# A third matmul group on the first 128 tokens at each stage change, with a narrower small piece and another order of the first transfers

## The chip, the cores and the metric

One core of one Trainium2 chip runs the whole program. The metric is the device time of one execution in microseconds (us). Five engines work side by side, each on its own list of instructions, in order: TensorE (matmuls and transposes; its weight loads are listed as PEld), VectorE (DVE), ScalarE (ACT), GpSimd (POOL) and SyncE (SP, which here issues the transfers from HBM). A difference of about 0.3%, some 3.4 us, is what runs of this kernel can tell from no change.

## The reference

Two layers, each over 256 tokens of width 1024, all in fp32:

```
for l in range(2):
    h   = rms_norm(x, norm_mix_pre[l])
    mix = hybrid_mixer(h, w_in[l], ...)          # 4 branches, gates, w_branch, w_out
    x   = x + rms_norm(mix, norm_mix_post[l])
    h   = rms_norm(x, norm_ffn_pre[l])
    x   = x + rms_norm(swiglu(h, w_ffn_in[l], w_ffn_out[l]), norm_ffn_post[l])

def swiglu(h, w_in, w_out):
    g, up = split(h @ w_in, 2);  return (silu(g) * up) @ w_out
```

The mixer multiplies h by w_in once and cuts the product into the inputs of four branches: a state-space branch, a gated softmax attention (fox), a block attention (moba) and one with selected keys (dsa). Their outputs go through w_branch, are weighted by sigmoid(h @ w_gate + b_gate), summed, and multiplied by w_out.

## The kernel before

Nearly all of the time is matmuls against weights that come from HBM once. A *chunk* is 1 MB of raw fp32 weights in SBUF. Each half of a chunk is split in two: `split_hi` (L303) lets ACT write whi, the weights in TensorE's fp32r form, and `split_lo` (L123, `sub_lo`) lets DVE write wlo, the remainder. The activations are split likewise into hh and hl, and each product is three matmuls: hh by whi, hl by whi, hh by wlo.

The work is a list of *quanta* in an order written out by hand. There are two forms. In `add_b` the weights stand in the array and 256 token columns pass by: 24 matmuls of 128x256 a quantum. In `add_a` 128 tokens stand in the array (the halves t=0 and t=1 of the 256) and 512 weight columns pass by: two chunks (kh=0, kh=1), each for both halves, so four quanta (kh, t) of 12 matmuls. `add_rows` does w_out and w_ffn_out; its last rows run for t=0 first and then for t=1, so that t=0 is done early.

The loop at the end of the program (L1100 to L1121) goes through the list. For each quantum it issues the loads (`load_to`), then the whi of the quanta up to HA=3 places ahead (`split_ahead`), then the wlo up to LA=2 ahead, then the quantum's matmuls. A chunk's `early` adds to both look-aheads. A program's engines get their instructions in that order, so a split that is emitted before a norm stands before it on its engine.

A *stage change* (`boundary`) happens three times: mixer to FFN in layer 0 (about 357 to 380 us), FFN to mixer (549 to 570) and mixer to FFN in layer 1 (905 to 928). There the result of one stage passes a norm, is added to x, passes the next stage's norm and is transposed. This runs per half t. `head` squares on ACT (junk, poss, L219) and multiplies on DVE (ny<-a,gain, L222); `body` adds to x (L226), squares again on ACT (junk, pnss, L234), multiplies (L237), takes the reciprocal root on POOL (pnr, L204) and scales on DVE (ny<-ny,pnr, L240); `tail_half` transposes ny on TensorE (eight 128x128, L268), writes hh on ACT (L279) and hl on DVE (L123). The next stage's first quanta are (0,0), (1,0) on t=0, then t=1's transposes (`st["t1"]`, hung before the third quantum as its `pre`), then (0,1), (1,1) on t=1.

Other places: the small piece of w_in (ik, dt, ff, iw; 84 columns laid out over 128, so its whi and wlo tiles are zeroed on POOL, L301 and L311), the start of the program (L155, L156, L1081 to L1088: SP issues x, grows, cst, then the first half chunks), and the FFN's columns (`ga_post`, `g_post`, `u_post`), where the first 256 columns of g and of u are form a and the rest form b.

Of the kernel before, what the change touches and what calls it, by code (L numbers as in the profile page):

```python
# [9 lines left out]
F32 = mybir.dt.float32  # L10
# [49 lines left out]
    return c  # L60


NS4 = 26
TAIL = 6
MID = 1
STEP = 3
HA = 3
LA = 2


class Chunk:
    def __init__(self, loads, pieces, zero=False):
        self.loads = loads
        self.pieces = pieces
        self.zero = zero
        self.raw = None
        self.early = 0
        self.hi = [None] * len(pieces)
        self.lo = [None] * len(pieces)


class Quantum:
    def __init__(self, chunk, pieces, emit):
        self.chunk = chunk
        self.pieces = pieces
        self.emit = emit
        self.pre = None
        self.ends = False


@with_exitstack
def kernel(ctx: ExitStack, tc: tile.TileContext, a, out):
# [11 lines left out]
    def gps():  # L104
        return pg.tile([P, 512], F32, name="g")
# [190 lines left out]
    def split_hi(c, i):  # L296
        if c.hi[i] is not None:
            return
        c.hi[i] = s4.tile([P, 1024], F32R, name="whi", tag="s4", bufs=NS4)
        if c.zero:  # L300
            G.memset(c.hi[i].bitcast(F32), 0.0)  # L301
        for src, dst in c.pieces[i]:
            A.activation(dst(c.hi[i]), src(c.raw), AF.Copy)  # L303

    def split_lo(c, i):
        split_hi(c, i)
        if c.lo[i] is not None:
            return
        c.lo[i] = s4.tile([P, 1024], F32R, name="wlo", tag="s4", bufs=NS4)
        if c.zero:  # L310
            G.memset(c.lo[i].bitcast(F32), 0.0)  # L311
        for src, dst in c.pieces[i]:
            sub_lo(dst(c.lo[i]), src(c.raw), dst(c.hi[i]))

# [42 lines left out]
    def small_chunk(w):  # L357
        def blk(lo, hi):
            return lambda r: kcols(r[:, :KT * P], KT)[:, :, lo:hi]

        def wsrc(c0, n):
            return w[:, c0:c0 + n].rearrange("(k p) c -> p k c", p=P)
        loads = [(blk(0, 64), wsrc(COL["ik"], 64)), (blk(64, 72), wsrc(COL["dt"], 8)),
                 (blk(72, 80), wsrc(COL["ff"], 8)), (blk(96, 100), wsrc(COL["iw"], 4))]

        def src(r):
            return blk(0, 64)(r).rearrange("p k (two j) -> p k j two", two=2)

# [9 lines left out]
    def emit_b(hi, lo, kt, hh, hl):  # L378
        o = gps()[:, :S]
# [8 lines left out]
    def add_b(chunk, n, post):  # L388
        chunks.append(chunk)
        for j in range(n):  # L390
            def emit(j=j):
                return post(j, emit_b(kcols(chunk.hi[j], KT), kcols(chunk.lo[j], KT), KT, *h_act()))
            quanta.append(Quantum(chunk, [j], emit))

    def add_a(w, cols, post, by_token):
        cs = [a_chunk(w, kh, cols) for kh in range(2)]
        chunks.extend(cs)
        acc = {}
        qs = []
        for kh, t in [(0, 0), (1, 0), (0, 1), (1, 1)] if by_token else [(0, 0), (0, 1), (1, 0), (1, 1)]:  # L400
            def emit(kh=kh, t=t):
                hh, hl = st["h"][kh]
                if kh == 0:
                    acc[t] = gps()
                wh = [kcols(p, 2) for p in cs[kh].hi]
                wl = [kcols(p, 2) for p in cs[kh].lo]
                for pc in range(2):
                    for n, (h, w_) in enumerate(((hh, wh), (hh, wl), (hl, wh))):
                        for k in range(2):
                            mm(acc[t], h[:, 2 * pc + k, t * P:(t + 1) * P], w_[pc][:, k, :],  # L410
                               kh + pc + n + k == 0, kh + pc + n + k == 5)
                if kh:
                    return post(t, acc[t])
            qs.append(Quantum(cs[kh], [0, 1], emit))
        quanta.extend(qs)
# [92 lines left out]
    def mixer(l):  # L508
# [99 lines left out]
        def agemm(key, first=False):  # L608
            cs, qs = add_a(w, [COL[key]], v_post(key), first and l > 0)
            if first:  # L610
                cs[0].early = cs[1].early = 2
                if l:
                    qs[2].pre = st["t1"]
                else:
                    qs[1].pre, qs[2].pre = st["t1"]

        agemm("mv", True)
        agemm("fv")
        add_b(small_chunk(w), 1, small_post)
# [77 lines left out]
    def gates_gen(l, L, sraw):  # L697
        pt = aps()
        for t in range(2):
            T.transpose(pt[:, t * P:(t + 1) * P], sraw[:, t * P:(t + 1) * P], ident)  # L700
        yield
        pv = pt[:, 0:2 * P].rearrange("p (t c) -> p t c", t=2)

# [7 lines left out]
        V.tensor_scalar(L["w16"], pv[:, :, 96:100], 1.0 / 16, None, op0=ALU.mult)  # L711
# [251 lines left out]
    def ffn(l):  # L963
# [26 lines left out]
        def ga_post(t, o):  # L990
            yield
            g = tp.tile([P, S], F32, name="gt", bufs=5)
            A.activation(g, o[:, 0:S], AF.Silu)
            yield
            u = t1k("hu")
            V.tensor_tensor(u, g, o[:, S:2 * S], op=ALU.mult)
            yield
            pt = aps()
            for j in range(2):
                T.transpose(pt[:, j * P:(j + 1) * P], u[:, j * P:(j + 1) * P], ident)  # L1000
            yield
            qs = slice(t * P, (t + 1) * P)
            hid_of(0)
            hh, hl = H[0]
            pv = pt[:, :S].rearrange("p (k q) -> p k q", k=2)
            A.activation(hh[:, 0:2, qs], pv, AF.Copy)
            yield
            sub_lo(hl[:, 0:2, qs], pv, hh[:, 0:2, qs])
# [142 lines left out]
```

## Time and profile before

| | |
|---|---|
| three runs | 1118.28, 1115.13, 1118.37 us (median 1118.28) |
| the profiled execution | 1115.65 us, its span 1113.6 us |
| TensorE busy | 1094.3 us, 98% of the span |
| DVE, ACT, POOL busy | 712.2, 588.4, 239.0 us (64%, 53%, 21%) |
| the chain that ended last | 81% TensorE, 12% DVE, 2% ACT |
| HBM | 169 GB/s over the span |

TensorE is busy nearly all the time, so time can only be won where it waits or by giving it less to do. Matmuls overlap in TensorE and their ends are modelled, so a wait is best read at the weight load of the instruction that waited (engine PEld), where the row names in brackets how long the engine had nothing to do and which instruction released it. In a timeline the first number is the start, the second the busy time of the whole group of equal instructions.

### The profile page before, as it was taken

The numbers are of one execution on the slowest core, as the hardware profiler recorded it, in microseconds if no ns is written. First come the engines' busy times: TensorE is split into PE (matmuls) and PEld (weight loads), VectorE is DVE, ScalarE is ACT, GpSimd is POOL, SyncE is SP. The second block draws the span as 40 slices with busy tenths as digits, with TensorE's granted clock in tenths as the row PEclk, the third lists the DMA queues.
The fourth block names the chain that finished last, engine by engine and source line by source line (L and its number), as shares of the span: only waits on it lengthen the run. The fifth ranks groups of instructions, "written<-read, shape, count | busy, mean of one in ns | idle before, by whom it ended". The sixth has DMA issues, their size and how long they took to land.

```text
span 1113.6 us, 20105 instructions
## 1 busy us (share of the span) xinstructions
PE 1094.3 (98%) x8067; PEld 1013.4 (91%) x8067; DVE 712.2 (64%) x1324; ACT 588.4 (53%) x1084; POOL 239.0 (21%) x277
## 2 busy tenths in 40 slices
PE   7999999999999999999999999999999999999997
PEld 5998989999999899998879999899999988999986
DVE  6799857554556755456478996666555576555542
ACT  6546764665445554445355576655644455444541
POOL 1332347113232100000014333451223120000000
PEclk9999999999999999999999999999999999999999
DMA  7744543444548355646654445343455664555651
GB/s 229 230 152 140 164 152 119 149 149 152 190 156 291 121 190 162 199 170 227 227 146 132 152 152 190 114 152 120 147 160 181 214 202 153 194 184 185 217 185 38
DMA packets 153920, 188.94 MB, mean 170 GB/s; under 512 B 12740, under 2 KB 129764, under 8 KB 153828
## 3 DMA queue, kind: packets, MB, share of 16 engines
q1 hardware_dynamic: 153828, 187.67, 51.5%
q8 instruction: 63, 1.03, 0.4%
q14 instruction: 29, 0.24, 0.1%
HBM read 186.61 MB, written 1.05 MB: 169 GB/s over the span
## 4 chain that ended last, share of the span: by engine, by line
PE 81%; DVE 12%; ACT 2%; issue 2%; DMA 2%; POOL 1%; SPq 1%; DVEq 0%; POOLq 0%; ACTq 0%
PE g L120 61%; PE a L120 18%; DVE wlo L123 4%; DVE cacc L581 2%; DMA raw<-in_w_in_dram 2%; PE a L836 1%; ACT whi L303 1%; ACT junk L234 1%; DVE iacc L790 1%; DVE iacc L782 1%; DVE sm L814 1%; POOL pnr L204 1%; DVE rsh L499 1%; DVE m L789 1%; DVE ny L240 0%
## 5 line engine op out<-in xcount | busy, mean ns | idle before, releaser
L123 DVE TENSOR_TENSOR wlo<-raw,whi 128x1024 fp32r<-128x1024 f32 (+2 forms) x386 | 443.1, 1168 | 116.9 <-ACT whi L303 97.4
L303 ACT ACTIVATE whi<-raw 128x1024 fp32r<-128x1024 f32 (+2 forms) x386 | 367.5, 986 | 66.0 <-DMA raw<-in_w_ffn_out_dram 24.1
L120 PE MATMUL g<-hh,whi 128*128 128x256 f32 x1776 | 254.0, 286 | 0.0
L120 PE MATMUL g<-hl,whi 128*128 128x256 f32 x1776 | 249.3, 283 | 0.0
L120 PE MATMUL g<-hh,wlo 128*128 128x256 f32 x1776 | 249.2, 283 | 0.0
L120 PEld LDWEIGHTS g<-hh,whi 128*128 128x128 f32 x1776 | 227.9, 191 | 8.0 <-DVE rc L826 1.3
L120 PEld LDWEIGHTS g<-hh,wlo 128*128 128x128 f32 x1776 | 229.1, 192 | 0.0
L120 PEld LDWEIGHTS g<-hl,whi 128*128 128x128 f32 x1776 | 229.0, 192 | 0.0
L830 POOL TENSOR_SCALAR pr<-pr,rc 128x128 f32<-128x128 f32 x96 | 71.3, 754 | 153.8 <-DVE rc L826 131.8
L639 ACT ACTIVATE gt<-g,par 128x256 f32<-128x256 f32 x64 | 30.4, 475 | 118.4 <-PE g L120 118.4
L659 POOL TENSOR_TENSOR mg<-mg,gt 128x256 f32<-128x256 f32 x48 | 53.8, 1128 | 123.9 <-DVE gt L653 122.5
L150 POOL TENSOR_SCALAR gain<-gain 128x1024 f32<-128x1024 f32 x4 | 4.3, 1082 | 336.7 <-DMA gain<-in_norm_mix_pre_dram 157.7
L983 DVE TENSOR_TENSOR hu<-gt,g 128x256 f32<-128x256 f32 x40 | 16.8, 421 | 87.0 <-PE g L120 87.0
L120 PE MATMUL a<-whi,hidh 128*128 128x512 f32 x176 | 55.6, 390 | 0.0
L120 PE MATMUL a<-whi,hidl 128*128 128x512 f32 x176 | 55.5, 389 | 0.0
L120 PE MATMUL a<-wlo,hidh 128*128 128x512 f32 x176 | 55.5, 389 | 0.0
L975 ACT ACTIVATE gt<-g 128x256 f32<-128x256 f32 x40 | 15.4, 384 | 67.8 <-PE g L120 67.8
L502 POOL TENSOR_TENSOR rsh<-rsh,cst 128x256 f32<-128x256 f32 (+1 forms) x38 | 29.5, 775 | 93.6 <-DVE rsh L499 93.6
L653 DVE SCALAR_TENSOR_TENSOR gt<-gt,g 128x256 f32<-128x256 f32 x48 | 20.0, 419 | 44.5 <-PE g L120 38.5
L821 ACT ACTIVATE pr<-sm,mn 128x128 f32<-128x128 f32 x96 | 42.5, 447 | 7.5 <-DVE mn L814 7.5
L120 PE MATMUL g<-whi,hh 128*128 128x512 f32 x128 | 40.6, 399 | 2.4 <-ACT hh L274 1.7
L985 ACT ACTIVATE hidh<-hu 128x256 fp32r<-128x256 f32 x40 | 16.7, 418 | 45.3 <-DVE hu L983 45.3
(209 smaller groups left out, 1322.7 us busy)
## 6 DMA issues: line engine op xcount, KB each, us to landing
raw<-in_w_ffn_in_dram SPq DMA_DIRECT2D x40, 1024.0 KB, 5.2
raw<-in_w_in_dram SPq DMA_DIRECT2D x38, 1024.0 KB, 5.0
raw<-in_w_gate_dram SPq DMA_DIRECT2D x32, 1024.0 KB, 5.5
raw<-in_w_ffn_out_dram SPq DMA_DIRECT2D x22, 1024.0 KB, 4.9
raw<-in_w_branch_dram SPq DMA_DIRECT2D x16, 1024.0 KB, 5.1
raw<-in_w_in_dram SPq DMA_DIRECT2D x24, 512.0 KB, 6.2
raw<-in_w_out_dram SPq DMA_DIRECT2D x8, 1024.0 KB, 7.2
raw<-in_w_ffn_in_dram SPq DMA_DIRECT2D x8, 512.0 KB, 5.0
```

The lines of the kernel that those rows point to most:

```text
L120: T.matmul(o, l, r, start=start, stop=stop)
L123: V.tensor_tensor(lo, src, hi.bitcast(F32), op=ALU.subtract)
L303: A.activation(dst(c.hi[i]), src(c.raw), AF.Copy)
L502: G.tensor_tensor(sh[:n], sh[:n], sin[:n], op=ALU.mult)
L581: V.scalar_tensor_tensor(ac[:, sft:], u[:, :S - sft], wcol(3 - sft), ac[:, sft:], op0=ALU.mult, op1=ALU.add)
L639: A.activation(th, o, AF.Tanh, bias=par[:, l, 40 + br * 8 + d:41 + br * 8 + d], scale=0.5)
L653: V.scalar_tensor_tensor(L["gt", d], L["gt", d], 1.0, os[j], op0=ALU.add, op1=ALU.mult)
L659: G.tensor_tensor(md, md, L["gt", d], op=ALU.add)
L821: A.activation(pr[b][:, sl], sm[b][:, sl], AF.Exp, bias=mn[b][:, t:t + 1], scale=-1.0, accum_out=ls[b][:, t:t + 1])
L830: G.tensor_scalar(pr[b][:, sl], pr[b][:, sl], rc[b][:, t:t + 1], 1.0, op0=ALU.mult, op1=ALU.mult)
L983: V.tensor_tensor(u, H["s", j], o, op=ALU.mult)
L985: A.activation(hh, u, AF.Copy)
```

## The change

- At the three stage changes (not at the program's start) two groups of form a are emitted together by `begin`: (0,0) and (1,0) of the first group and (0,0) of the second on t=0, with t=1's transposes between the two halves of that third quantum (`mid`), then the five others. The second group's first chunk also has early=2, and the quanta of t=1 in `add_rows` load one chunk further (`after`).
- So the FFN's second 256 columns of g and u become form a instead of b. In mixer 1 the two groups are mv and fv, which were form a before.
- The small piece is 84 columns wide: its matmuls have 84 weight columns, its transposes 84 partitions; the zeroing is gone, and two of its three split pieces are one.
- At the start grows and the first part of cst are issued by ACT instead of SP, and the second half of x goes before the first chunk's second half.
- NS4, the number of 128x1024 tiles that whi, wlo, ny and others share, goes from 26 to 28.

```diff
-NS4 = 26
+NS4 = 28
+NSMALL = 84
-    nc.sync.dma_start(g_rows, a["norm_mix_pre"][0].rearrange("(k p) -> k p", p=P))
-    nc.sync.dma_start(cst[:, 0:P], a["cst"][:, 0:P])
+    nc.scalar.dma_start(g_rows, a["norm_mix_pre"][0].rearrange("(k p) -> k p", p=P))
+    nc.scalar.dma_start(cst[:, 0:P], a["cst"][:, 0:P])
...
-        if c.zero:
-            G.memset(c.hi[i].bitcast(F32), 0.0)
...
-                 (blk(72, 80), wsrc(COL["ff"], 8)), (blk(96, 100), wsrc(COL["iw"], 4))]
+                 (blk(72, 80), wsrc(COL["ff"], 8)), (blk(80, 84), wsrc(COL["iw"], 4))]
...
+    def group_a(w, cols, post):
...
+                    for pc in range(2):
+                        if pc and q.mid is not None:
+                            q.mid()
...
+    def begin(w, *groups):
+        (ca, qa), (cb, qb) = (group_a(w, *g) for g in groups)
+        chunks.extend(ca + cb)
+        quanta.extend([qa[0, 0], qa[1, 0], qb[0, 0], qa[0, 1], qa[1, 1], qb[0, 1], qb[1, 0], qb[1, 1]])
+        for c in (ca[0], ca[1], cb[0]):
+            c.early = 2
+        qb[0, 0].mid = st["t1"]
...
                 quanta[-1].ends = c == nch - 1
+                if t:
+                    quanta[-1].after = cs[-1]
...
+        if l:
+            begin(w, ([COL["mv"]], v_post("mv")), ([COL["fv"]], v_post("fv")))
...
-        cs, qs = add_a(w, [0, FFN], ga_post, True)
-        cs[0].early = cs[1].early = 2
-        qs[2].pre = st["t1"]
-        for c in range(1, FFN // S):
+        begin(w, ([0, FFN], ga_post(0)), ([S, FFN + S], ga_post(1)))
+        for c in range(2, FFN // S):
...
-    for step in "0 1 x 2 3".split():
+    for step in "0 x 1 2 3".split():
...
-        load_to(cidx[id(q.chunk)] + 3)
+        load_to(cidx[id(q.chunk)] + 3 if q.after is None else cidx[id(q.after)] + 4)
```

How this moves the instructions is seen at the first stage change. On ACT, from the squares of the old stage's t=0 to the first activation of the FFN (whi are the next chunks' splits, pnss the squares of the next norm, hh the activations after the transposes), before:

```order
L219 ACTIVATE junk,poss<-a 128x512 x2
L303 ACTIVATE whi<-raw 128x1024 x2
L234 ACTIVATE junk,pnss<-x 128x512 x2
L219 ACTIVATE junk,poss<-a 128x512
L279 ACTIVATE hh<-a 128x4x128 x2
L219 ACTIVATE junk,poss<-a 128x512
L234 ACTIVATE junk,pnss<-x 128x512 x2
L303 ACTIVATE whi<-raw 128x1024
L279 ACTIVATE hh<-a 128x4x128 x2
```

And after the change (line numbers are higher by two):

```order
L221 ACTIVATE junk,poss<-a 128x512 x2
L303 ACTIVATE whi<-raw 128x1024 x4
L236 ACTIVATE junk,pnss<-x 128x512 x2
L221 ACTIVATE junk,poss<-a 128x512
L281 ACTIVATE hh<-a 128x4x128 x2
L221 ACTIVATE junk,poss<-a 128x512
L236 ACTIVATE junk,pnss<-x 128x512 x2
L281 ACTIVATE hh<-a 128x4x128 x2
```

Two more whi stand ahead of t=0's squares, and the one ahead of t=1's hh is gone. On DVE, from t=0's addition to x to t=1's hl, before:

```order
L226 SCALAR_TENSOR_TENSOR x<-ny,por,x 128x512 x2
L237 TENSOR_TENSOR ny<-x,gain 128x512
L202 TENSOR_SCALAR pnm<-pnss 128x1
L237 TENSOR_TENSOR ny<-x,gain 128x512
L240 TENSOR_SCALAR ny<-ny,pnr 128x512 x2
L123 TENSOR_TENSOR wlo<-raw,whi 128x1024 x2
L222 TENSOR_TENSOR ny<-a,gain 128x512
L123 TENSOR_TENSOR hl<-a,hh 128x4x128 x2
L202 TENSOR_SCALAR pom<-poss 128x1
L222 TENSOR_TENSOR ny<-a,gain 128x512
```

After:

```order
L228 SCALAR_TENSOR_TENSOR x<-ny,por,x 128x512 x2
L239 TENSOR_TENSOR ny<-x,gain 128x512
L204 TENSOR_SCALAR pnm<-pnss 128x1
L239 TENSOR_TENSOR ny<-x,gain 128x512
L242 TENSOR_SCALAR ny<-ny,pnr 128x512 x2
L125 TENSOR_TENSOR wlo<-raw,whi 128x1024 x4
L224 TENSOR_TENSOR ny<-a,gain 128x512
L125 TENSOR_TENSOR hl<-a,hh 128x4x128 x2
L204 TENSOR_SCALAR pom<-poss 128x1
L224 TENSOR_TENSOR ny<-a,gain 128x512
```

Two more wlo stand between t=0's scaled ny and its hl. On TensorE, from the last matmuls of quantum (1,0) on, before:

```order
L120 MATMUL g<-wlo,hh 128x512 x2
L120 MATMUL g<-whi,hl 128x512 x2
L268 MATMUL a<-cst,ny 128x128 x8
L120 MATMUL g<-whi,hh 128x512 x2
L120 MATMUL g<-wlo,hh 128x512 x2
```

After, where a and cst are the transposes' output and identity:

```order
L122 MATMUL g<-wlo,hh 128x512 x2
L122 MATMUL g<-whi,hl 128x512 x2
L122 MATMUL g<-whi,hh 128x512 x2
L122 MATMUL g<-wlo,hh 128x512 x2
L122 MATMUL g<-whi,hl 128x512 x2
L270 MATMUL a<-cst,ny 128x128 x8
L122 MATMUL g<-whi,hh 128x512 x2
L122 MATMUL g<-wlo,hh 128x512 x2
```

Six more matmuls on t=0 stand ahead of t=1's transposes, and six more (the second half of the third quantum) between them and the first matmul that needs t=1's hh.

## Rows read from the trace of the kernel before

**Rows 1.** The chain that ended last: start us, us, what (x instructions)

```profile
275.55 72.18 PE g L120 x600
...
362.14 1.72 ACT whi L303 x2
...
367.58 2.27 DVE wlo L123 x2
...
895.98 13.64 PE a L120 x60
```

**Rows 2.** Busy time by windows: window, length, PE, PEld, DVE, ACT, POOL, clock, DMA, GB/s

```profile
100.00:120.00 20.00, 18.05 (x145) 16.56 (x145) 19.58 (x60) 15.47 (x40) 8.17 (x8) 1.00 0.49 158
357.00:380.00 23.00, 22.10 (x105) 17.87 (x104) 16.65 (x28) 12.07 (x25) 2.96 (x4) 1.00 0.40 129
560.00:575.00 15.00, 12.52 (x58) 9.80 (x57) 13.09 (x18) 7.50 (x14) 3.20 (x4) 1.00 0.27 42
905.00:930.00 25.00, 24.11 (x114) 19.48 (x113) 18.94 (x31) 13.80 (x27) 2.97 (x4) 1.00 0.39 126
```

**Rows 3.** Timeline of PEld, first stage change: start, busy, line, [wait, releaser]

```profile
367.77 1.02 PEld L268 LDWEIGHTS a<-cst,ny 128*128 128x128 f32 x8
...
371.10 0.30 PEld L120 LDWEIGHTS g<-whi,hl 128*128 128x128 f32 x2 [0.21 <-DVE hl L123]
...
376.58 0.86 PEld L268 LDWEIGHTS a<-cst,ny 128*128 128x128 f32 x8 [1.08 <-DVE ny L240]
377.93 0.30 PEld L120 LDWEIGHTS g<-whi,hh 128*128 128x128 f32 x2 [0.49 <-ACT hh L279]
```

**Rows 4.** Timeline of ACT, first stage change

```profile
362.04 2.00 ACT L303 ACTIVATE whi<-raw 128x1024 fp32r<-128x1024 f32 x2
363.94 0.62 ACT L234 ACTIVATE junk<-x 128x512 f32<-128x512 f32 x1
```

**Rows 5.** Timeline of DVE, first stage change

```profile
366.70 0.88 DVE L240 TENSOR_SCALAR ny<-ny,pnr 128x512 f32<-128x512 f32 x2 [0.45 <-POOL pnr L204]
...
370.37 1.28 DVE L123 TENSOR_TENSOR hl<-a,hh 128x512 fp32r<-128x512 f32 x2
...
376.04 0.88 DVE L240 TENSOR_SCALAR ny<-ny,pnr 128x512 f32<-128x512 f32 x2 [0.44 <-POOL pnr L204]
```

**Rows 6.** Timeline of PEld, second stage change

```profile
560.78 0.30 PEld L120 LDWEIGHTS g<-whi,hl 128*128 128x128 f32 x2 [0.25 <-DVE hl L123]
...
567.88 0.86 PEld L268 LDWEIGHTS a<-cst,ny 128*128 128x128 f32 x8 [2.65 <-DVE ny L240]
569.22 0.30 PEld L120 LDWEIGHTS g<-whi,hh 128*128 128x128 f32 x2 [0.49 <-ACT hh L279]
```

**Rows 7.** Timelines of DVE and POOL, second stage change

```profile
565.79 2.42 DVE L240 TENSOR_SCALAR ny<-ny,pnr 128x512 f32<-128x512 f32 x2 [0.44 <-POOL pnr L204]
...
565.70 0.95 POOL L301 MEMSET whi<- 128x1024 f32 x1
```

**Rows 8.** DMA issues of 352 to 356 us: count, KB each, us to landing

```profile
raw<-in_w_ffn_in_dram SPq DMA_DIRECT2D x1, 1024.0 KB, 7.2
```

**Rows 9.** Timeline of SP at the start: issue of transfers

```profile
1.63 0.37 SPq L155 DMA_DIRECT2D grows<-in_norm_mix_pre_dram  x1
...
2.43 0.94 SPq L294 DMA_DIRECT2D raw<-in_w_in_dram  x2
```

**Rows 10.** Timeline of ACT at the start

```profile
3.39 0.63 ACT L234 ACTIVATE junk<-x 128x512 f32<-128x512 f32 x1 [1.39 <-DMA x<-in_x_dram]
...
7.57 1.06 ACT L303 ACTIVATE whi<-raw 128x1024 fp32r<-128x1024 f32 x1 [2.68 <-DMA raw<-in_w_in_dram]
```

**Rows 11.** Timelines of DVE, POOL and PEld at the start, t=1's norm

```profile
12.88 1.78 DVE L257 TENSOR_SCALAR ny<-x,pnr 128x512 f32<-128x512 f32 x2 [0.67 <-POOL pnr L204]
...
13.04 0.95 POOL L301 MEMSET whi<- 128x1024 f32 x1
...
14.32 0.85 PEld L268 LDWEIGHTS a<-cst,ny 128*128 128x128 f32 x8 [1.46 <-DVE ny L257]
```

More of the change, by code (lines that the diff above doesn't have):

```diff
@@ L71, with __init__ @@
 class Chunk:
-    def __init__(self, loads, pieces, zero=False):
+    def __init__(self, loads, pieces):
         self.loads = loads
         self.pieces = pieces
-        self.zero = zero
         self.raw = None
@@ L87, in __init__ @@
         self.pre = None
+        self.mid = None
+        self.after = None
         self.ends = False
@@ L309, in split_lo @@
         c.lo[i] = s4.tile([P, 1024], F32R, name="wlo", tag="s4", bufs=NS4)
-        if c.zero:
-            G.memset(c.lo[i].bitcast(F32), 0.0)
         for src, dst in c.pieces[i]:
@@ L370, in dst @@
             return blk(0, 64)(r).rearrange("p k (j two) -> p k j two", two=2)
-        p1, p2 = blk(64, 80), blk(96, 100)
-        return Chunk(loads, [[(src, dst), (p1, p1), (p2, p2)]], zero=True)
+        p1 = blk(64, 84)
+        return Chunk(loads, [[(src, dst), (p1, p1)]])
     def h_act():
@@ L376, in h_act, with emit_b @@
         return (lambda k: hs[k // 4][0][:, k % 4, :]), (lambda k: hs[k // 4][1][:, k % 4, :])
-    def emit_b(hi, lo, kt, hh, hl):
-        o = gps()[:, :S]
+    def emit_b(hi, lo, kt, hh, hl, m=P):
+        o = gps()[:m, :S]
         for k in range(kt):
@@ L386, in emit_b, with add_b @@
         return o
-    def add_b(chunk, n, post):
+    def add_b(chunk, n, post, m=P):
         chunks.append(chunk)
@@ L391, in emit @@
             def emit(j=j):
-                return post(j, emit_b(kcols(chunk.hi[j], KT), kcols(chunk.lo[j], KT), KT, *h_act()))
+                return post(j, emit_b(kcols(chunk.hi[j], KT)[:, :, :m], kcols(chunk.lo[j], KT)[:, :, :m], KT,
+                                      *h_act(), m))
             quanta.append(Quantum(chunk, [j], emit))
-    def add_a(w, cols, post, by_token):
+    def group_a(w, cols, post):
         cs = [a_chunk(w, kh, cols) for kh in range(2)]
-        chunks.extend(cs)
[L398 to L415, printed above, removed]
-        return cs, qs
@@ new lines, in group_a, with emit, run @@
+        acc = {}
+        qs = {}
+        for kh in range(2):
+            for t in range(2):
+                def emit(q, kh=kh, t=t):
+                    hh, hl = st["h"][kh]
+                    if kh == 0:
+                        acc[t] = gps()
+                    wh = [kcols(p, 2) for p in cs[kh].hi]
+                    wl = [kcols(p, 2) for p in cs[kh].lo]
+                    for pc in range(2):
+                        if pc and q.mid is not None:
+                            q.mid()
+                        for n, (h, w_) in enumerate(((hh, wh), (hh, wl), (hl, wh))):
+                            for k in range(2):
+                                mm(acc[t], h[:, 2 * pc + k, t * P:(t + 1) * P], w_[pc][:, k, :],
+                                   kh + pc + n + k == 0, kh + pc + n + k == 5)
+                    if kh:
+                        return post(t, acc[t])
+                q = Quantum(cs[kh], [0, 1], None)
+                def run(emit=emit, q=q):
+                    return emit(q=q)
+                q.emit = run
+                qs[kh, t] = q
@@ new lines, in group_a, with add_a @@
+        return cs, qs
+    def add_a(w, cols, post):
+        cs, qs = group_a(w, cols, post)
+        chunks.extend(cs)
+        quanta.extend(qs[o] for o in ((0, 0), (0, 1), (1, 0), (1, 1)))
+        return cs, qs
+    def begin(w, *groups):
[5 more added lines that the diff above has]
+        qb[0, 0].mid = st["t1"]
@@ L514, in small_post @@
             sraw = t1k("sraw")
-            A.activation(sraw, o, AF.Copy)
+            A.activation(sraw[:NSMALL], o, AF.Copy)
             yield from rope(o[0:64], [(L["ik"][0:64], LOWER)], 64)
@@ L606, in bgemm, with agemm @@
                 add_b(cols_chunk(w, COL[key] + c * S, S, KT, perm), 2, post(2 * c))
-        def agemm(key, first=False):
-            cs, qs = add_a(w, [COL[key]], v_post(key), first and l > 0)
-            if first:
-                cs[0].early = cs[1].early = 2
-                if l:
-                    qs[2].pre = st["t1"]
[L614 to L619, printed above, removed]
+        def agemm(key):
+            return add_a(w, [COL[key]], v_post(key))
+        if l:
+            begin(w, ([COL["mv"]], v_post("mv")), ([COL["fv"]], v_post("fv")))
+        else:
+            cs, qs = agemm("mv")
+            cs[0].early = cs[1].early = 2
+            qs[0, 1].pre, qs[1, 0].pre = st["t1"]
+            agemm("fv")
+        add_b(small_chunk(w), 1, small_post, NSMALL)
         bgemm("iq", lambda b: rope_post("iq", b, lambda: start(index_gen(l, L)), 2), True, 2)
@@ L699, in gates_gen @@
         for t in range(2):
-            T.transpose(pt[:, t * P:(t + 1) * P], sraw[:, t * P:(t + 1) * P], ident)
+            T.transpose(pt[:, t * P:t * P + NSMALL], sraw[:NSMALL, t * P:(t + 1) * P], ident[:NSMALL, :NSMALL])
         yield
@@ L710, in gates_gen @@
         L["w16"] = tp.tile([P, 2, 4], F32, name="w16")
-        V.tensor_scalar(L["w16"], pv[:, :, 96:100], 1.0 / 16, None, op0=ALU.mult)
+        V.tensor_scalar(L["w16"], pv[:, :, 80:84], 1.0 / 16, None, op0=ALU.mult)
         flags.add(("w16", l))
@@ L988, in u_post, with ga_post, f @@
             return f
[L990 to L1008, printed above, removed]
-        cs, qs = add_a(w, [0, FFN], ga_post, True)
-        cs[0].early = cs[1].early = 2
-        qs[2].pre = st["t1"]
-        for c in range(1, FFN // S):
+        def ga_post(c):
+            def f(t, o):
+                yield
+                g = tp.tile([P, S], F32, name="gt", bufs=5)
+                A.activation(g, o[:, 0:S], AF.Silu)
+                yield
+                u = t1k("hu")
+                V.tensor_tensor(u, g, o[:, S:2 * S], op=ALU.mult)
+                yield
+                pt = aps()
+                for j in range(2):
+                    T.transpose(pt[:, j * P:(j + 1) * P], u[:, j * P:(j + 1) * P], ident)
+                yield
+                qs, ks = slice(t * P, (t + 1) * P), slice(2 * c, 2 * c + 2)
+                hid_of(0)
+                hh, hl = H[0]
+                pv = pt[:, :S].rearrange("p (k q) -> p k q", k=2)
+                A.activation(hh[:, ks, qs], pv, AF.Copy)
+                yield
+                sub_lo(hl[:, ks, qs], pv, hh[:, ks, qs])
+            return f
+        begin(w, ([0, FFN], ga_post(0)), ([S, FFN + S], ga_post(1)))
+        for c in range(2, FFN // S):
             add_b(cols_chunk(w, c * S, S, KT), 2, g_post)
```

## The prediction

> **What bounds the kernel now.** I read the chain of waits first. It is matmuls nearly throughout, back to back: 600 of 128x256 take 72.18 us, so 0.120 us each, and 60 of 128x512 take 13.64 us, so 0.227 us each [rows 1]. Where TensorE never waits, only less work helps; so I looked next, in the busy time by windows, for the places where it does wait [rows 2]. The three stage changes leave 23.00 - 22.10 = 0.90, 15.00 - 12.52 = 2.48 and 25.00 - 24.11 = 0.89 us idle. Mixer 0 has one more hole: 1.95 us in 100 to 120 us, where DVE is busy 19.58 of 20 us. The rest of the loss is at the two ends of the program.
>
> Then I read one stage change engine by engine. In the first, TensorE reaches t=0's transposes at 367.77 and does not wait. It waits 0.21 us for t=0's hl at 371.10, then 1.08 us for t=1's scaled ny and 0.49 us for t=1's hh [rows 3]. The reader is to see what the chain of waits goes through there: two whi on ACT at 362.14 (ahead of t=0's squares) and two wlo on DVE at 367.58 (ahead of t=0's hl) [rows 1]. So splits that stand ahead of the norm are on the path already; one more there is paid in full. That decides the forecast.
>
> **The change part by part.**
>
> *The splits of the third group, on t=0's chain.* The order lists show two more whi on ACT ahead of t=0's squares and two more wlo on DVE ahead of t=0's hl. A pair of whi takes 363.94 - 362.04 = 1.90 us [rows 4], a pair of wlo 2.27 us [rows 1]. ACT goes from the whi into the squares without a wait, so the squares come 1.90 us later, the scaled ny at 366.70 + 1.90 = 368.60 [rows 5]. t=1's rows say how soon transposes follow: 376.58 - 376.04 = 0.54 us [rows 3, 5]. So t=0's transposes can start at 369.14, where TensorE was ready at 367.77: a new wait of 1.37 us. DVE then runs four wlo instead of two, so t=0's hl starts 1.90 + 2.27 = 4.17 us later, at 374.54 instead of 370.37 [rows 5], and the matmul that waits for it moves from 371.10 to 375.27. This is 2.8 us more of waiting after the 1.37.
>
> *What the third group then covers.* t=1's chain stands behind these same instructions on DVE, so it is 4.17 us late too: its transposes can start at 376.58 + 4.17 = 380.75. From the hl matmul to the end of the two first quanta TensorE had 376.58 - 1.08 - 371.10 = 4.40 us of work [rows 3]; now it has six matmuls more, 6 x 0.227 = 1.36 us. It comes to the transposes at 375.27 + 4.40 + 1.36 = 381.03, and they are ready. The 1.08 us wait is gone. The transposes take 0.86 us; t=1's hh is ready 377.93 - 376.58 = 1.35 us after their start, and the 1.36 us of the second half cover it: the 0.49 us wait is gone too. t=1's first matmul starts at 381.03 + 0.86 + 1.36 = 383.25. By then 2.72 us of work is done that came later before. Against 377.93 the stage change costs 383.25 - 2.72 - 377.93 = +2.60 us.
>
> *The two other stage changes.* The third shows the same idle time as the first (0.89 against 0.90 us [rows 2]), so I put it at +2.60 as well. The second waits longer for t=1's ny, 2.65 us [rows 6], because DVE's scaling took 2.42 us instead of 0.88 while POOL zeroed the small piece's whi, from 565.70 on [rows 5, 7]; that zeroing goes. The hl matmul moves from 560.78 to 564.95; 567.88 - 2.65 - 560.78 = 4.45 us of work and 1.36 more end at 570.76; ny is ready at 565.79 + 0.54 + 4.17 = 570.50. So 570.76 + 0.86 + 1.36 - 2.72 - 569.22 = +1.04 us. Together +6.24 us. The bounds: if both pairs of splits fell into time in which nobody waits, the waits would go at no price, -1.57 - 3.14 - 1.57 = -6.3 us; if the next chunk came late as well, more than +6.24. I take the middle case as worked out, since the chain names both pairs' places.
>
> *The data for it.* The third transfer at 352 to 356 us, 1 MB of w_ffn_in, is issued at about 354.4 in the same place of SP's list and lands 7.2 us later [rows 8], near 361.6; ACT wants it at 363.94. Its cover is 2.3 us. If it is gone, each us late is a us of t=0's chain.
>
> *FFN columns.* 96 matmuls of 256 columns, 96 x 0.120 = 11.5 us, become 48 of 512, 48 x 0.227 = 10.9 us, with four transposes more (eight took 0.86 us [rows 3], so 0.43). Per FFN -0.2, together -0.4 us, between 0 and -1.2.
>
> *Start.* SP issued grows at 1.63 and the first half chunk at 2.43 [rows 9]; with grows and cst on ACT the half chunk goes 0.80 us sooner. ACT's first whi waited 2.68 us for it, to 7.57 [rows 10]. ACT's own two issues (as long as SP's, 0.37 us the one shown) fit before its first square at 3.39, which waited 1.39 us. I take -0.80 us, between 0 and -1.35. At t=1's norm the scaling took 1.78 us while POOL zeroed the same whi (13.04), and TensorE waited 1.46 us for it at 14.32 [rows 11]; without the zeroing 0.88, so -0.90, of which at least -0.3 should stay. Together -1.7, between -0.3 and -2.3. It reaches the end only through the stretch up to 120 us in which DVE is full; I take it that DVE's work starts sooner as well.
>
> The Trainium skill ("DMA: Bandwidth & Descriptors", section "Queues, rings and completion order") says that each DMA engine takes one ring's descriptors in ring order and goes round between the queues that have work. By that rule the first half chunk, behind x alone on SP's queue, would gain more than its 0.80, up to the 1.35 at which the hh before it decides, and the sum would be 0.55 us lower. Rows 10 do not tell: the wait for raw ends once only.
>
> *The rest.* 84 columns instead of 128: the same 24 matmuls of 256 moving columns, so nothing on TensorE; one split piece less per layer on ACT and DVE, and the smaller transposes, under 0.3 us. The 28 tiles cost nothing, and no row shows a wait for such a tile.
>
> The sum: +6.24 - 0.4 - 1.7 = +4.1 us, 1119.8 us against the profiled 1115.65. That execution lies below the median of the runs shown, 1118.28; from the median the sum gives 1122.4. I say 1122.
>
> **The rivals.**
>
> *A: the third group costs nothing and only fills.* Place: ACT at 362 and DVE at 367.5; the mechanism is that t=0's chain does not hang on its queue there (the additional splits run while ACT and DVE have nothing else, and DVE's hl is not needed in time). Then all waits of the three changes go: -6.3 - 0.4 - 1.7 = -8.4 us, 1110. It decides if TensorE came to t=0's transposes at least 1.4 us later than now, and to the first hl matmul 4 us later. For it speaks that TensorE's first chunk could wait for something else; against it, the chain of waits and the missing wait between whi and the square.
>
> *B: half of it.* Only ACT's pair delays, since the wlo turn out short or find a gap. Then the hl matmul comes at 373.00, the transposes at 378.76 against ready at 378.48, and the first and third change cost +0.33, the second -1.23: together -0.6, with the rest -2.7 us, 1115.6, within the bound. Against it: DVE runs its list in order, and hl stands behind the wlo in it.
>
> *C: the clock falls in the new waits.* The waits would be 1.4 and 2.8 us; the longest in these rows, 2.65 us, left the granted clock of its window at 1.00 [rows 2, 6], its upper level, 2.4 GHz. If it fell to 1.2 GHz for the 4.4 us that follow, each change would cost some 4.4 us more, +13 in all: 1135. The Trainium skill ("TensorE: Matmul & The Clock Gate", Part 1) has the slow clock as the default to which idleness leads back; the row at 2.65 us agrees with no fall there.
>
> *D: the start's gain is lost and the third chunk's data is late by 1 us.* +6.2 - 0.4 - 0.3 + 3 = +8.5: 1126.8. Slower as well.
>
> **How the numbers follow.** 0.3%, about 3.4 us, is what a measurement can tell from no change. The forecast has 0.55 with its own range 1119 to 1125, C 0.04, D 0.06, B 0.2, A 0.15. The forecast's +4.1 lies little above the bound: a fifth of its weight counts as the same. A and a fifth of B are faster: 0.19. The rest of B and that part of the forecast are within: 0.27. Slower: 0.54. The range leaves out C and the lower half of A and reaches from 1111 to 1126.
>
> **What would show it.** In the profile of the changed kernel, at each stage change: ACT runs four whi before t=0's squares; TensorE waits about 1.4 us at t=0's transposes for ny and about 3 us at the first hl matmul for hl; no wait at t=1's transposes nor at its first hh matmul; the granted clock stays at 1.00. At the second, DVE's scaling takes 0.88 us. At the start ACT's first whi is at about 6.8 us. If the new wait for hl is under 1 us, rival A or B is right and the forecast wrong; if ACT waits for raw before its third whi, D.

## The result, and the profile after

The changed kernel takes 1125.85 us (median of four runs, 1125.37 to 1127.39), the kernel before beside it 1118.13 us (1115.13 to 1118.37): a ratio of 1.0079, 95% interval 1.0063 to 1.0095. It is slower, and inside the range by 0.15 us, but by about twice what was forecast: +7.7 us between the medians, where the sum gave +4.1 and the 1122 that was stated is 3.7 above the median of before. On another chip (after_again below) it was 1.0076 (1.0061 to 1.0090).

The profiled execution took 1125.37 us with a span of 1123.6 us, 10.0 us longer than the one of before. Where it was lost can be read instruction by instruction, since both kernels load the same weights into TensorE in nearly the same order: the start of a load in the timeline of after, less the start of the same load in the timeline of before, is the delay gathered up to there. It is +0.54 us at 92 us, +2.04 from 140 us to the first stage change, +4.66 after it and the FFN's columns (at 407 us of before), +7.34 after the second stage change (at 596) and +9.93 after the third (at 980).

The first stage change on PEld, which answers to [rows 3]; ACT and DVE follow, which answer to [rows 4, 5]:

```profile
371.24 0.86 PEld L270 LDWEIGHTS a<-cst,ny 128*128 128x128 f32 x8 [1.46 <-issue]
...
377.31 0.30 PEld L122 LDWEIGHTS g<-whi,hl 128*128 128x128 f32 x2 [3.10 <-DVE hl L125]
...
383.13 1.02 PEld L270 LDWEIGHTS a<-cst,ny 128*128 128x128 f32 x8
...
385.38 0.41 PEld L122 LDWEIGHTS g<-whi,hh 128*128 128x128 f32 x2
```

```profile
364.08 3.89 ACT L303 ACTIVATE whi<-raw 128x1024 fp32r<-128x1024 f32 x4
367.87 0.62 ACT L236 ACTIVATE junk<-x 128x512 f32<-128x512 f32 x1
```

```profile
370.63 0.88 DVE L242 TENSOR_SCALAR ny<-ny,pnr 128x512 f32<-128x512 f32 x2 [0.45 <-POOL pnr L206]
371.43 4.62 DVE L125 TENSOR_TENSOR wlo<-raw,whi 128x1024 fp32r<-128x1024 f32 x4
375.97 0.68 DVE L224 TENSOR_TENSOR ny<-a,gain 128x512 f32<-128x512 f32 x1
```

The two waits that the kernel before had at t=1's transposes and at its first matmul (1.08 and 0.49 us) are gone: the rows at 383.13 and 385.38, the latter t=1's first matmul, have no bracket. In their place stand 1.46 us at t=0's transposes and 3.10 us at t=0's hl, because ACT spends 3.89 us on four whi and DVE 4.62 us on four wlo, where each had two. (The row with 1.46 us names no instruction that ended the wait; DVE's scaling of t=0's ny, at 370.63, stands 0.61 us ahead of it, and the wait is gone in a_noearly, whose splits stand elsewhere.)

The second stage change shows the same two waits, and DVE's scaling at 0.88 instead of 2.42 us [rows 6, 7]. But behind the wait the weight loads take 0.76 us a pair instead of 0.41, and the window's granted clock is 0.90, where the window of before had 1.00 [rows 2]. Weight loads on PEld, then the window (length, PE, PEld, DVE, ACT, POOL, clock, DMA share, GB/s):

```profile
563.49 0.86 PEld L270 LDWEIGHTS a<-cst,ny 128*128 128x128 f32 x8 [1.46 <-issue]
...
569.56 0.30 PEld L122 LDWEIGHTS g<-whi,hl 128*128 128x128 f32 x2 [3.10 <-DVE hl L125]
569.90 0.41 PEld L122 LDWEIGHTS g<-whi,hh 128*128 128x128 f32 x2
...
571.50 0.76 PEld L122 LDWEIGHTS g<-whi,hh 128*128 128x128 f32 x2
```

```profile
8.00:20.00 12.00, 10.37 (x33) 7.46 (x34) 9.03 (x19) 10.21 (x22) 0.81 (x2) 0.72 0.93 347
100.00:120.00 20.00, 18.03 (x133) 16.80 (x132) 19.58 (x58) 15.09 (x41) 8.17 (x8) 0.91 0.49 158
359.00:388.00 29.00, 25.27 (x119) 20.51 (x118) 20.08 (x31) 14.39 (x27) 2.97 (x4) 1.00 0.43 140
563.00:580.00 17.00, 13.82 (x61) 11.17 (x62) 12.82 (x20) 5.61 (x14) 1.41 (x2) 0.90 0.38 83
914.00:942.00 28.00, 24.27 (x115) 19.67 (x114) 19.62 (x30) 14.84 (x28) 2.96 (x4) 1.00 0.40 131
```

At the stage changes TensorE is idle 3.73, 3.18 and 3.73 us in these windows (0.90, 2.48 and 0.89 before). The granted clock was at its lower level, 1.2 GHz, for part of three windows: at the start (0.72), behind the hole at 111 us (0.91), and behind the second stage change (0.90). At the start ACT's first whi came no sooner (7.57 before [rows 10]) and its second one waits, though the first half chunk was issued at 1.63 instead of 2.43 us. DVE's scaling at t=1's norm takes 0.89 us instead of 1.78 [rows 11]. Issue on SP, ACT, DVE:

```profile
1.63 0.43 SPq L296 DMA_DIRECT2D raw<-in_w_in_dram  x1
...
7.77 1.06 ACT L303 ACTIVATE whi<-raw 128x1024 fp32r<-128x1024 f32 x1 [2.54 <-DMA raw<-in_w_in_dram]
...
10.43 1.06 ACT L303 ACTIVATE whi<-raw 128x1024 fp32r<-128x1024 f32 x1 [0.57 <-DMA raw<-in_w_in_dram]
...
13.77 0.89 DVE L259 TENSOR_SCALAR ny<-x,pnr 128x512 f32<-128x512 f32 x2 [0.67 <-POOL pnr L206]
```

### The profile page after: what moved, and what is told of

It reads as the page before. It is cut to its first block, busy times and chain, and to the rows that moved or that the text cites. A ratio compares the mean times of both kernels' runs of the same rounds, so it can differ in the third digit from the quotient of the medians.

```text
span 1123.6 us, 19946 instructions
## 1 busy us (share of the span) xinstructions
PE 1099.0 (98%) x7979; PEld 1013.6 (90%) x7979; DVE 709.1 (63%) x1322; ACT 587.6 (52%) x1082; POOL 233.1 (21%) x273
## 3 DMA queue, kind: packets, MB, share of 16 engines
HBM read 186.61 MB, written 1.05 MB: 167 GB/s over the span
## 4 chain that ended last, share of the span: by engine, by line
PE 88%; DVE 8%; ACT 2%; issue 1%; DMA 1%; POOL 0%; SPq 0%; DVEq 0%; POOLq 0%; ACTq 0%
PE g L122 67%; PE a L122 18%; DVE wlo L125 3%; DVE cacc L602 2%; PE a L856 1%; ACT whi L303 1%; DMA raw<-in_w_in_dram 1%; DVE iacc L810 1%; DVE sm L834 1%; DVE m L809 0%; PE a L270 0%; ACT junk L236 0%; DVE iacc L802 0%; DVE xsc L588 0%; POOL pnr L206 0%
## 5 line engine op out<-in xcount | busy, mean ns | idle before, releaser
L125 DVE TENSOR_TENSOR wlo<-raw,whi 128x1024 fp32r<-128x1024 f32 (+1 forms) x384 | 441.7, 1171 | 108.7 <-ACT whi L303 92.7
L303 ACT ACTIVATE whi<-raw 128x1024 fp32r<-128x1024 f32 (+1 forms) x384 | 366.5, 990 | 56.6 <-DMA raw<-in_w_ffn_out_dram 31.3
L122 PE MATMUL g<-hh,whi 128*128 128x256 f32 (+1 forms) x1712 | 245.3, 286 | 0.0
L122 PE MATMUL g<-hl,whi 128*128 128x256 f32 (+1 forms) x1712 | 241.0, 284 | 0.0
L122 PE MATMUL g<-hh,wlo 128*128 128x256 f32 (+1 forms) x1712 | 240.7, 283 | 0.0
L122 PEld LDWEIGHTS g<-hh,whi 128*128 128x128 f32 (+1 forms) x1712 | 219.6, 191 | 8.0 <-DVE rc L846 1.3
L122 PEld LDWEIGHTS g<-hl,whi 128*128 128x128 f32 (+1 forms) x1712 | 221.4, 192 | 0.0
L122 PEld LDWEIGHTS g<-hh,wlo 128*128 128x128 f32 (+1 forms) x1712 | 221.3, 192 | 0.0
L122 PE MATMUL g<-whi,hl 128*128 128x512 f32 x160 | 51.0, 401 | 8.0 <-DVE hl L125 8.0
L122 PE MATMUL g<-wlo,hh 128*128 128x512 f32 x160 | 51.2, 402 | 0.3 <-DVE wlo L125 0.2
```

What stands on the lines that cost most here:

```text
L122: T.matmul(o, l, r, start=start, stop=stop)
L125: V.tensor_tensor(lo, src, hi.bitcast(F32), op=ALU.subtract)
```

## The experiments

The theory after this result: the splits on t=0's chain cost what was forecast; each fall of the granted clock adds some 1.6 us; and the gain at the start does not exist or does not reach the end. The rivals stand in each expectation. The delays that the runs gathered against the profile of before, in us, by the method above (the columns are the stretches between 0, 92, 140, 407, 596 and 980 us of before; each row of a kernel is one profiled execution):

| kernel | start | 111 us | 1st change | 2nd | 3rd | end |
|---|---|---|---|---|---|---|
| forecast | -1.7 | 0 | +2.4 | +1.0 | +2.4 | +4.1 |
| changed | +0.54 | +1.50 | +2.62 | +2.68 | +2.59 | +9.93 |
| changed, again | +0.18 | 0.0 | +4.24 | +1.04 | +4.20 | +9.64 |
| a_fill | -0.19 | 0.0 | +2.60 | +1.04 | +2.56 | +6.01 |
| a_noearly | -0.45 | +1.69 | +0.48 | -0.97 | +0.44 | +1.20 |
| b_start | +0.87 | +1.46 | 0.0 | -0.64 | 0.0 | +1.69 |
| b_narrow | -0.44 | +0.19 | 0.0 | -1.29 | 0.0 | -1.51 |
| g1 | -0.74 | +1.69 | -1.56 | -3.09 | -1.61 | -5.31 |
| b_early | +0.22 | +1.66 | -0.14 | -1.31 | -0.17 | +0.26 |
| g2 | -0.12 | +0.19 | -1.58 | -3.07 | -1.59 | -6.16 |
| b_fill | +0.20 | +0.19 | 0.0 | +0.87 | 0.0 | +1.29 |

**The third group without its early splits (a_noearly).** Changed kernel, one line:

```diff
-        for c in (ca[0], ca[1], cb[0]):
+        for c in ca:
```

> The changed kernel, but the third group's first chunk has no additional look-ahead: its two whi come behind t=0's squares on ACT and its two wlo behind t=1's scaling on DVE. Theory (the splits on t=0's chain are the cost): TensorE waits neither for t=0's scaled ny nor over 0.3 us for t=0's hl; it waits some 2.1 us for wlo in the third quantum instead. First and third stage change +0.55 us each against the kernel before (the changed kernel has +2.6), the second -1.1 (it has +2.7, part of that the clock), no half clock at the second: 7.9 us less than the changed kernel, about 1118. Rival (the third group itself costs, by its order on TensorE or its PSUM): the stage changes keep their +2.6 and the time stays at 1125 to 1126.

Measured: 1117.23 us, ratio to before 1.0006 (0.9995 to 1.0017). TensorE's waits at the first stage change:

```profile
369.01 1.02 PEld L270 LDWEIGHTS a<-cst,ny 128*128 128x128 f32 x8
...
372.34 0.30 PEld L122 LDWEIGHTS g<-whi,hl 128*128 128x128 f32 x2 [0.21 <-DVE hl L125]
...
379.35 0.30 PEld L122 LDWEIGHTS g<-wlo,hh 128*128 128x128 f32 x2 [2.15 <-DVE wlo L125]
380.16 1.03 PEld L270 LDWEIGHTS a<-cst,ny 128*128 128x128 f32 x8
```

Both new waits are gone, and the wait for wlo that was expected at about 2.1 us is 2.15. The three stage changes gave +0.48, -0.97 and +0.44 us (expected +0.55, -1.1, +0.55). So the third group costs little by itself (the half microsecond left at the first and third is that wait for wlo); what the changed kernel lost there it lost by the place of two whi and two wlo.

**Matmuls that keep the clock up in the waits (a_fill).**

```diff
+                warm_up(5)
                 B[0].tail(st["h"])
...
+                            if q.fill and pc + (2 - n) == 0:
+                                warm_up(q.fill)
...
+        qa[0, 0].fill = 12
```

> The changed kernel with 5 idle-running bf16 matmuls ahead of t=0's transposes and 12 ahead of the first matmul with hl at each stage change: they fill about 1.1 of the 1.46 us and 2.6 of the 3.10 us in which TensorE waits, and nothing waits for them. Theory (the half clock after the second stage change comes from these waits): the granted clock stays at 1.00 there and the second stage change falls from +2.7 to about +1.0, the others stay at +2.6; 1124.2, 1.6 less than the changed kernel. Rival (the clock falls for another reason, or the fall costs nothing): clock and time as in the changed kernel, 1125.9.

Measured: 1122.35 us, ratio 1.0046 (1.0031 to 1.0061); the four mean granted clocks 0.997 to 0.999, where the changed kernel's first four were 0.993 to 0.995. The windows at the three stage changes (PE counts the idle matmuls as busy):

```profile
369.00:385.00 16.00, 15.93 (x79) 12.03 (x79) 13.53 (x21) 6.46 (x13) 1.48 (x2) 1.00 0.42 133
561.00:577.00 16.00, 15.93 (x79) 11.84 (x78) 13.04 (x21) 6.25 (x13) 1.41 (x2) 1.00 0.41 89
921.00:937.00 16.00, 15.94 (x78) 12.06 (x79) 13.54 (x21) 6.58 (x13) 1.48 (x2) 1.00 0.41 133
```

The clock is whole (1.00, never at its lower level) in this profile, and the second change costs +1.04 us, the forecast's number to the hundredth. The idle matmuls do nothing but run; t=0's hl is as late as in the changed kernel. So the falls at the stage changes come from the waits. By the ratios the filling is worth 0.3%, some 3.3 to 3.7 us, twice the 1.6 expected: an execution has one or two such falls, as the next run shows.

**The changed kernel again (after_again).** No edit.

> The changed kernel once more, unaltered, beside the others, for its own scatter. Theory (the waits at the stage changes cost the same each time, and the clock falls in some places only by the moment of the execution): the three stage changes again at +2.6, +1.0 (or +2.7 with a half clock behind it) and +2.6 against the kernel before; ratio about 1.007; mean granted clocks of 0.993 to 0.997. Rival (its first profile was a special one): stage changes that differ by more than 0.3 us where the clock is whole.

Measured: 1125.37 us, ratio 1.0076 (1.0061 to 1.0090). The stage changes did not cost the same again, for this time the second change had a whole clock and cost +1.04, and the first and third had a low one and cost 4.24 and 4.20 us:

```profile
370.00:385.00 15.00, 12.34 (x54) 9.84 (x52) 11.05 (x18) 4.49 (x11) 1.48 (x2) 0.89 0.45 141
569.00:584.00 15.00, 14.72 (x69) 12.27 (x70) 9.76 (x17) 6.56 (x13) 1.41 (x2) 1.00 0.41 110
922.00:940.00 18.00, 14.43 (x64) 11.64 (x64) 13.62 (x21) 6.59 (x14) 1.71 (x3) 0.91 0.36 117
```

Equal waits (1.46, then 3.10 us at all three places in both profiles) lower the clock in one place and not in another, from execution to execution; a fall costs 4.24 - 2.60 = 1.6 us. The hole at 111 us behaves alike: TensorE waits 2.08 to 2.34 us there in nine profiles, five of them have the low clock behind it and lose 1.46 to 1.69 us, and before has not, with 2.15 us. What decides it was not tested.

**The start alone (b_start).** The kernel before, with

```diff
-    nc.sync.dma_start(g_rows, ...    # and cst[:, 0:P]
+    nc.scalar.dma_start(g_rows, ...
-    for step in "0 1 x 2 3".split():
+    for step in "0 x 1 2 3".split():
```

> The kernel before with the start of the changed one alone: grows and cst issued by ACT, the second half of x ahead of the first chunk's second half. Theory (the transfers share one bandwidth, so the half chunk that is issued 0.8 us sooner lands no sooner, and its second half later): ACT's first whi at 7.6 to 7.8 us, the second about 1 us later than before, TensorE's unbroken stretch begins 0.5 to 1 us later, and the half clock appears in the first 20 us: the end is +0.6 to +2.5 us later than before by the span. Rival (a queue's transfers land in their order of issue): first whi at 6.8, the end 0.8 us sooner.

Measured: 1117.20 us, ratio 1.0004 (0.9993 to 1.0016): no difference that can be told. The profiles tell a little more. The first whi began at 7.77, 8.00, 7.67, 6.83 and 7.75 us in the five profiles with the new order, and at 7.57, 6.83, 6.37, 7.23, 6.59 and 6.52 in the six with the old: on the mean 7.60 against 6.85, with a scatter of 1.2 us within either set. So the half chunk that is issued 0.80 us sooner lands no sooner, and on the mean 0.75 us later. Its second half is late too, since x goes ahead of it:

```profile
7.75 1.06 ACT L303 ACTIVATE whi<-raw 128x1024 fp32r<-128x1024 f32 x1 [2.28 <-DMA raw<-in_w_in_dram]
...
10.43 1.06 ACT L303 ACTIVATE whi<-raw 128x1024 fp32r<-128x1024 f32 x1 [0.58 <-DMA raw<-in_w_in_dram]
```

The rival (landing in the order of issue, so the first whi at 6.8) has the order right and the time wrong. The loads of SP's queue do land as they were issued: in the changed kernel the first half chunk at 7.7 us, x at 9.1 and the second half chunk at 10.4 (1.63 + 6.1, 2.10 + 7.0 and 2.61 + 7.8, issue and time to landing), in the kernel before the two half chunks at 7.5 and 8.9 (2.43 + 5.1, 2.90 + 6.0). From 3 to 6 us the transfers moved 224 to 279 GB/s in the new order and 269 to 292 in the old; the one profile of the new order with 279 is the one whose first whi began at 6.83. Why the new order mostly moves less there was not tested. The half clock stood at 111 us in this profile, not at the start as expected.

**The narrow piece alone (b_narrow).** The kernel before, with NSMALL's edits and without the zeroing.

> The kernel before with the narrow small piece alone (84 columns, no zeroing on POOL, two split pieces instead of three). Theory (the zeroing on POOL slowed DVE's scaling): the scaling of t=1 at the start takes 0.88 instead of 1.78 us, at the second stage change 0.88 instead of 2.42, and TensorE's wait there falls from 2.65 to about 1.1 us: -1.5 us there, -0.9 us at the start if nothing else is late, together -2.4. Rival (something else is late behind it): less than 0.5 us gained in all.

Measured: 1115.80 us, ratio 0.9983 (0.9973 to 0.9993), a small gain. At the second stage change it is as expected: DVE's scaling takes 0.88 us, TensorE's wait is 1.14 instead of 2.65 us, and the change gives -1.29 us:

```profile
565.86 0.88 DVE L240 TENSOR_SCALAR ny<-ny,pnr 128x512 f32<-128x512 f32 x2 [0.44 <-POOL pnr L204]
...
566.40 0.86 PEld L268 LDWEIGHTS a<-cst,ny 128*128 128x128 f32 x8 [1.14 <-DVE ny L240]
```

Near 43 us TensorE ran 1.49 us ahead of before (0.74 of it because the first half chunk happened to land sooner, first whi at 6.83 instead of 7.57), and lost 1.05 of it in one new wait at 57 us, for the results that DVE makes there (sg), and more later:

```profile
57.32 0.55 PEld L120 LDWEIGHTS a<-cst,sg 128*16 128x16 f32 x6 [1.22 <-DVE sg L727]
...
111.18 0.52 PEld L120 LDWEIGHTS a<-mk,mq 64*128 64x128 f32 x6 [2.33 <-DVE mn L810]
```

This is the stretch in which DVE is full. A start that is sooner by 1.5 us is worth 0.25 behind it, so of the 2.4 us expected 1.5 are left at the end.

**The splits taken off the norm's chain (g1).** Changed kernel with the old start, and

```diff
-        for c in (ca[0], ca[1], cb[0]):
-            c.early = 2
+        ca[0].early, ca[1].early, cb[0].early = 2, 3, 1
...
-        for d, q in enumerate(quanta[i:i + ahead + 3]):
+        for d, q in enumerate(quanta[i:i + ahead + 4]):
```

The first group's second chunk is now split while ACT and DVE wait for t=0's last matmuls, and the third group's first chunk in the places that became free.

> The changed kernel with the start of the kernel before, and with the splits taken off the norm's chain: the first group's second chunk is split one quantum sooner (in time in which ACT and DVE wait for t=0's last matmuls), and the third group's first chunk has its whi behind t=0's squares and its wlo behind t=0's scaling. Theory (only the place of the splits made the change slow): TensorE waits at no transposes of the stage changes; -1.6, -3.1 and -1.6 us there against the kernel before, -0.2 per FFN, -0.2 of the start's -1.5 left: about -6.9 us, ratio 0.994. Rival 1 (the first group's second chunk lands too late for the sooner place: ACT waits for raw ahead of t=0's squares): 0 to +3 us a stage change. Rival 2 (the third group costs by itself): 0 or slower at each.

Measured: 1110.51 us (1109.43 to 1111.12), ratio 0.9941 (0.9928 to 0.9954): faster than the kernel before and than the changed one. The three changes gave -1.56, -3.09 and -1.61 us (expected -1.8, -3.1 and -1.8 with the columns), and TensorE is busy throughout:

```profile
357.00:380.00 23.00, 23.00 (x111) 19.08 (x110) 18.51 (x30) 11.80 (x25) 2.97 (x4) 1.00 0.59 194
559.00:575.00 16.00, 16.00 (x75) 13.16 (x75) 10.63 (x18) 7.39 (x15) 1.41 (x2) 1.00 0.34 103
901.00:926.00 25.00, 25.00 (x120) 20.75 (x119) 20.50 (x32) 14.21 (x27) 2.97 (x4) 1.00 0.53 174
```

**The sooner splits without the third group (b_early).** The kernel before with the narrow piece and the first group's second chunk at early=3 (at the program's start too), the loop's look-ahead one quantum longer as in g1.

> The kernel before with the narrow small piece and with the first group's second chunk split one quantum sooner, without the third group. Theory (t=1's chain then begins as soon as t=0's hl is done, and is bound by TensorE's last matmuls of t=1): t=1's transposes some 0.6 us sooner, TensorE still waits about 0.5 us for them and 0.49 for hh: -0.6, -2.0 (with the zeroing gone) and -0.6 us, start -0.3: -3.5 us, ratio 0.997. Rival (all the splits before t=0's hl were on the path, so t=0 and t=1 both come 2 us sooner): -1.6, -3.1, -1.6 us as with the third group, ratio 0.994, and the third group brings nothing.

Measured: 1115.36 us, ratio 0.9985 (0.9974 to 0.9996), as b_narrow. The stage changes gave -0.14, -1.31 and -0.17 us, less than the -0.6, -2.0 and -0.6 expected. Its trace says why: t=1's chain begins with the square of TensorE's last product, 0.52 us after DVE is free, and that comes hardly sooner (at 371.56 in the kernel before, which this profile trails by 1.88 us here).

```profile
371.47 1.28 DVE L123 TENSOR_TENSOR hl<-a,hh 128x512 fp32r<-128x512 f32 x2
373.27 0.21 DVE L202 TENSOR_SCALAR pom<-poss 128x1 f32<-128x1 f32 x1 [0.52 <-ACT junk L219]
```

So free DVE time alone is worth little. With g1 beside it, it is the matmuls of the third group on t=0 that fill the wait, and the sooner splits make room for the group's own.

**Filling the hole at 111 us (g2 and b_fill).** g1, and the kernel before, each with nine idle matmuls ahead of a score product of the block attention:

```diff
+                if fill and t == 0 and b == 1:
+                    warm_up(fill)
...
+                               9 if (l, br, i) == (0, 2, 2) else 0)
```

> The version with the splits off the norm's chain (g1), and 9 idle-running bf16 matmuls in the wait of mixer 0 at about 111 us (before the second score product of the third unit of the block attention, where TensorE waits 2.3 us for DVE). Theory (the half clock behind that wait, 3.4 us long, comes from the wait and costs about 1.5 us where an execution has it): no half clock there, mean granted clocks of 0.999, 1.5 us less than g1: about 1109, ratio 0.993. Rival (the clock falls there for another reason, or its fall is hidden because DVE sets the pace there): clock or time as in g1, 1110.5.

> The kernel before with the same 9 matmuls in the wait of mixer 0 at about 111 us. Theory (the scatter of the kernel before, 1115 to 1118 us, is in good part the half clock behind this wait): mean granted clocks of 0.998 to 0.999 in nearly all executions, the median 1 to 1.5 us lower, about 1115.2, the fastest as before. Rival (the scatter has another source): median and scatter as before.

Measured: 1109.82 us for g2, ratio 0.9938 (0.9925 to 0.9952), which g1's interval does not tell from g1; 1116.40 us for b_fill, ratio 0.9994 (0.9985 to 1.0003). The idle matmuls stood one unit too soon, at 98 us instead of 111, and put TensorE back by 2.5 us there; DVE sets the pace here, so the hole closed all the same and the 2.5 us were not lost (TensorE busy 20.00 of 20 us in 100 to 120, clock 1.00), and three of g2's five clocks were 0.999 against 0.997 in all of g1's. For the kernel before the expected 1 to 1.5 us did not show in the median. In its profile the clock fell elsewhere, behind the second stage change's old wait (here 1.80 and 0.75 us for the two halves of the scaled ny):

```profile
567.41 0.42 PEld L268 LDWEIGHTS a<-cst,ny 128*128 128x128 f32 x4 [1.80 <-DVE ny L240]
568.58 0.72 PEld L268 LDWEIGHTS a<-cst,ny 128*128 128x128 f32 x4 [0.75 <-DVE ny L240]
...
560.00:578.00 18.00, 16.12 (x68) 12.77 (x67) 13.91 (x19) 9.17 (x17) 3.48 (x4) 0.91 0.37 86
```

## Where the prediction was right, and where it failed

The direction, and the mechanism at the three stage changes, were right. The size was not, because two terms of the sum failed. The start was put at -1.7 us and measured about +0.2. The clock's falls were put at nothing and measured 1.6 us each, in one or two places of an execution. With the falls at the stage changes filled (a_fill) the kernel is still 5.7 us above before (1122.35 against 1116.65), where +4.1 was forecast: within the scatter of the runs that is the start and the 0.4 us by which the stage changes cost more. The rest, up to the 7.7 to 8.9 us measured, is the clock. That 1125.85 still lies under 1126 is luck: the forecast's own range ended at 1125.

- **The splits on t=0's chain: right.** New waits of 1.46 and 3.10 us, forecast 1.37 and 3.0 (2.8 more than the 0.21 that was there); t=0's hl matmul 377.31 - 371.10 - 2.04 (the delay brought along) = 4.17 us late, forecast 4.17. t=1's first matmul stands at 385.38 - 2.04 = 383.34, forecast 383.25.
- **What the third group covers, and the stage changes: right.** With a whole clock they cost 2.60, 1.04 and 2.56 us with the FFN's columns (forecast 2.4, 1.04, 2.4). The columns gain about 0.1 us an FFN instead of 0.2. The data was in time: ACT went into the third whi without a wait. So rivals B (half the cost) and D (late data) are out, though D had the start's gain lost, as it was.
- **The start: wrong, the first step that failed.** The prediction took -1.7 us, between -0.3 and -2.3, and let it reach the end. In the five profiles with the new order the delay at 92 us was +0.54, +0.18, -0.19, -0.45 and +0.87, about +0.2 on the mean; in the six with the old order it was -0.15 on the mean. Its first part, -0.80 us, was worked out as if a transfer that is issued sooner landed sooner by as much. The half chunk landed no sooner, on the mean 0.75 us later. The Trainium skill ("DMA: Bandwidth & Descriptors", "Queues, rings and completion order") has each DMA engine take one ring's descriptors in ring order; the landings at 7.7, 9.1 and 10.4 us agree with that order. What the prediction made of it, that the first half chunk gains more than its 0.80, is not borne out, and why the first landing was late stays open. The start's second part, the scaling without the zeroing, is there (0.89 us instead of 1.78) and is swallowed by DVE's full stretch, as b_narrow shows. The prediction had read this stretch (19.58 of 20 us) and taken the friendly answer.
- **The clock: the second step that failed.** Rival C was given 0.04 and a price of 13 us. Its mechanism is real; its price was too high (1.6 us a fall, in one or two of three places), its chance much too low. The failed inference is that one row, 2.65 us at a granted clock of 1.00, shows that such a wait leaves the clock alone: b_fill has that wait in two pieces, 1.80 and 0.75 us, with 0.91 in its window. The Trainium skill ("TensorE: Matmul & The Clock Gate", Part 1) has the slow clock as the default, to which an idle TensorE goes back. The traces agree that it goes back behind waits; they add that equal waits do it in some executions and not in others.
- **The base.** The profiled execution of before had a whole clock (mean 0.999), as few of its runs have: of the 25 beside a_noearly, from 1114.79 to 1119.64 us, five had 0.999, the others 0.994 to 0.997. So 9.9 us between the profiles are 7.7 to 8.9 between medians.
- **Sum.** Stage changes 2.60 + 1.04 + 2.56 = 6.2 us, about 0.2 at the start, and one or two falls of the clock of 1.6 us more than before has (an estimate from the mean clocks, 0.993 to 0.996 against mostly 0.997): 8 to 9.6 us, against 7.7 to 8.9 measured. The forecast had 5.8, less 1.7.
- **Rival A** was given its low chance for the right reason: the splits were on the chain. With them moved, g1 has A's gain at each stage change.

## What to carry to other kernels

Filler work for a wait is only as good as the place where its preparation stands: what engines do for it must not stand in front of the chain that the wait is for. The list of each engine in order, beside the chain of waits, told that here before a run, to 0.1 us. Discount a gain that lies ahead of a stretch in which another engine is full, and do not take one execution's whole clock as proof that a wait is harmless. And an earlier issue of a load need not be an earlier landing.

## What was not expected of the hardware

- A 512 KB transfer that was issued 0.80 us sooner, with others behind it and small ones on a second queue, completed no sooner: on the mean 0.75 us later (five profiles against six, with a scatter of 1.2 us in either set), though the queue's loads landed in the order of their issue.
- The granted clock fell behind equal waits of 3.10 us in some executions and not in others, behind waits of 2.08 to 2.34 us in five profiles of nine, and once behind 1.80 and 0.75 us; seventeen idle-running matmuls in the waits of 1.46 and 3.10 us kept it at 1.00 in the profile that has them.
